# One diffusion layer in split fp32: weights stored in load order, and another opening order

## The chip, the cores and the metric

The kernel runs on one core of one Trainium2 chip. The metric is the device time of one execution in microseconds (us), the median of the runs shown. TensorE is called PE in the profile, VectorE DVE, ScalarE ACT, GpSimd POOL, SyncE SP; PEld is PE's weight load, which can run beside a matmul. SPq is SP's stream of issued transfers.

## The reference

One layer over 512 latent tokens and 128 context tokens, model width 1024. Cut to what the change touches:

```python
mod = (jax.nn.silu(cond) @ w_ada + b_ada)[:, None, :]
sh1, sc1, g1, sh2, sc2, g2 = jnp.split(mod, 6, axis=-1)
h = _rms(x, norm_mix) * (1 + sc1) + sh1
mix, k, v = _mixer(h, rope, ctx_k, ctx_v, w_in, q_norm, k_norm, conv_w,
                   attn_out_norm, conv_out_norm, w_out)
x = x + g1 * mix
h2 = _rms(x, norm_ffn) * (1 + sc2) + sh2
gate, up = jnp.split(h2 @ w_gate_up, 2, axis=-1)
x = x + g2 * ((jax.nn.silu(gate) * up) @ w_down)
```

`cond` is one vector for the latent tokens and another for the context tokens. The columns of `w_in` are q (512), k and v (256) and three blocks of 512 of a gated convolution. Inside `_mixer` stand attention (8 query heads, 2 key heads, one softmax over 640 keys) and the convolution.

## The kernel before, in words

**Arithmetic.** Every large product is made in three matmuls: an operand is split into a rounded part (`hH`, `wh`) and a rest (`hL`, `wl`), and `mm3` (lines 154 to 157) adds hH·wh, hH·wl and hL·wh in one PSUM bank. A weight tile of 128 partitions by 1024 floats (512 KB) is loaded into `wf`, rounded by ACT into `wh` (`w_hi`, line 542), and DVE makes `wl` (`w_lo`, line 549).

**Tiles.** There are five token tiles of 128 tokens, 0 to 3 latent, 4 the context. Eight slices `k` of 128 channels make the width.

**Stages.** The opening (0 to 59.6 us of the trace) loads the tokens, norms them, transposes them, makes the modulation of the first norm and computes q for all tiles. After it come keys and values, attention with the convolution's matmuls between (to about 250 us), the output projection, and the feed-forward part to the end. Only the opening's order of work is changed.

**The opening, step by step.** The string `P1SEQ` lists its steps by hand; PE, DVE, ACT, POOL and SP execute what they issue in that order, so an engine that waits at one step holds all its later ones. A digit is a tile or a slice:

- `r t`: ACT squares and sums token tile `x` (line 501), DVE scales the sum (L163), POOL takes the power -0.5 (L165). `s t`: DVE multiplies the tile by it (L507).
- `x t`: PE transposes the tile, eight blocks of 128x128 (L468). `e t i a|d`: ACT (L473) or DVE (L475) copies half `i` of it from PSUM to `xT`.
- `a k`: 16 small matmuls of the two conditioning vectors `cp` with the loaded slices `af` of `w_ada` (L394). `b k`: DVE copies the sum to `res` (L439). `m k`: two transposes (L446), a reduction (L448) and three small DVE operations make `modA` and `modB`, a scale and a shift per channel.
- `h k c`: ACT and DVE turn `xT` into `hH` and `hL` for all latent tiles (c=0) or the context tile (c=1) of slice k (L486 to L493, L151, L152).
- `q k t`: three matmuls of 512 columns for slice k and tile t (L155 to L157). `w`, `l`: rounding of the next weight tile. `d n`: n dummy matmuls on the identity (`spin`, L523). `v0`, `v1`: PE transposes bias, gain and filter vectors that POOL loaded as rows (L401, L553), DVE copies them to `vec`. `E t`: q of tile t leaves PSUM.

**Queues.** All large loads are issued by SP in the order of the string `LOADS` (x: a token tile, A: slices of `w_ada`, W: a weight tile, C: the cached keys and values). A transfer is cut into the runs that are contiguous in device memory: 4 KB per partition for a token tile, 512 bytes for `af`, the convolution's and the gate/up weights, 2 KB for q, `w_out` and `w_down`. `af` has four buffers (`AFB`), so the load of slice k+2 waits for step `a` of slice k; `wf` has three. At most eight transfers of SP are outstanding.

**PSUM.** In the opening, tag `s` has two buffers of two banks, `t` and `c` two banks each; one bank of `c` holds q of the context tile from first to last, so all `a` steps use the other.

Of the kernel before, what the change touches and what calls it, by code (L numbers as in the profile page):

```python
# [9 lines left out]
F32 = mybir.dt.float32  # L10
F32R = mybir.dt.float32r
AF = mybir.ActivationFunctionType
# [3 lines left out]
P = 128  # L16
D = 1024
# [15 lines left out]
P1SEQ = ('d11 r0 s0 x0 r1 s1 r2 e00d x1 s2 e01d r3 v0 d4 x2 s3 e20a a0 e10d b0 e11d e21d x3 m0 d4 w e30a h00y l n0 '  # L33
# [4 lines left out]
XB = 3  # L38
# [49 lines left out]
LOADS = 'xxxxAWxAAWAAWAAAWCWWWW'  # L88
# [3 lines left out]
def build(ctx, tc, x_prompt, x_sample, c, cache_k, cache_v, c_ctx, norm_mix, norm_ffn, w_ada, b_ada,  # L92
          w_in, q_norm, k_norm, conv_w, attn_out_norm, conv_out_norm, w_out, w_gate_up, w_down,
          rope_c, rope_s, o_prompt, o_sample, o_k, o_v):
# [43 lines left out]
    def PS2():  # L138
        return PB((P, 2, 512), tag="s")
# [33 lines left out]
    open_pool("B0", "left", "crow rows rows2 res x xT hF af")  # L173
# [5 lines left out]
    wi = w_in[0].rearrange("(k p) n -> p k n", p=P)  # L179
    wa = w_ada[0].rearrange("(k p) n -> p k n", p=P)  # L180
    wo = w_out[0].rearrange("(k p) n -> p k n", p=P)
    wg = w_gate_up[0].rearrange("(k p) n -> p k n", p=P)
    wd = w_down[0].rearrange("(k p) n -> p k n", p=P)
# [89 lines left out]
    for j in range(4):  # L273
        plan(("q", j), wi[:, 2 * j:2 * j + 2, O_Q:O_Q + 512])
    for h in range(2):
        plan(("kv", h), wi[:, 4 * h:4 * h + 4, O_K:O_K + 256])
    ada_steps = [(sec, j, h) for sec, j in ADA for h in range(4)]
    for n, (off, ct) in enumerate(CONV + [(None, 0)]):
        if off is not None:
            plan(("conv", off, ct), wi[:, :, off + ct * P:off + (ct + 1) * P])  # L280
        for sec, j, h in ada_steps[2 * n - 2:2 * n if off is not None else None] if n else ():
            col = sec * D + j * 512
            plan(("ada", sec, j, h), wa[:, 2 * h:2 * h + 2, col:col + 512], 1, "a")
    for j in range(2):
        for kp in range(4):
            plan(("o", j, kp), wo[:, 2 * kp:2 * kp + 2, j * 512:(j + 1) * 512], 2 * j, "w", V_AON + 2 * kp)
        for kp in range(0 if j else 4):
            plan(("ada", 5, j, kp), wa[:, 2 * kp:2 * kp + 2, 5 * D + j * 512:5 * D + (j + 1) * 512], 2, "f")
# [6 lines left out]
    def plan_raw(f, x, ph=3):  # L295
        col = f * P + (DFF if x == "u" else 0)
        plan((x, f), wg[:, :, col:col + P], ph, "f")
# [6 lines left out]
    for gi, grp in enumerate(GROUPS):  # L304
        for f in grp:
            ph = 2 if f < NPLAIN else 3
            plan_raw(f, "g", ph)
            plan_raw(f, "u", ph)
            plan_ops(f, PLAIN if f < NPLAIN else PRODS, ph)
        for j in range(2):  # L310
            for i0 in range(0, len(grp), 2):
                n = len(grp[i0:i0 + 2])
                plan(("d", grp[i0], j), wd[:, grp[i0]:grp[i0] + n, j * 512:(j + 1) * 512], 2)
                if gi == 0 and j == 0:
                    for kp in G2KP[i0 // 2]:
                        plan(("ada", 5, 1, kp), wa[:, 2 * kp:2 * kp + 2, 5 * D + 512:6 * D], 2, "f")


    crow = T("crow", (16, P))
    sp.dma_start(crow[0:8, :], c[0].rearrange("(r q) -> r q", q=P))  # L320
    sp.dma_start(crow[8:16, :], c_ctx.rearrange("(r q) -> r q", q=P))
# [20 lines left out]
    rows, rows2 = T("rows", (64, P)), T("rows2", (20, P))  # L342
    pool.dma_start(rows[0:48, :], b_ada[0].rearrange("(r q) -> r q", q=P))
    pool.dma_start(rows[48:56, :], norm_mix[0].rearrange("(r q) -> r q", q=P))
    pool.dma_start(rows[56:64, :], norm_ffn[0].rearrange("(r q) -> r q", q=P))
# [50 lines left out]
    vec = T("vec", (P, 84))  # L396
    nb = T("nb", (P, 2, KD))

    def vec_do():
        vps = PB((P, 64))  # L400
        pe.transpose(vps, rows, ident[:64, :64])  # L401
        dve.tensor_copy(vec[:, 0:64], vps)
# [60 lines left out]
    def xT_do(t):  # L463

        both = PS2() if t < XB else None
        xps[t] = [both[:, i] if t < XB else PB() for i in range(2)]
        for k in range(KD):
            pe.transpose(xps[t][k // 4][:, k % 4 * P:(k % 4 + 1) * P], xs[t][:, k * P:(k + 1) * P], ident)  # L468

    def xT_evict(t, i, e):  # L470
        dst, src = xT[:, 4 * i:4 * i + 4, t * P:(t + 1) * P], xps[t][i].rearrange("p (k q) -> p k q", q=P)
        if e == "a":
            act.activation(dst, src, AF.Copy)  # L473
        else:
            dve.tensor_copy(dst, src)  # L475
# [21 lines left out]

    def x_norm(t):
        junk = T2((P, D), mybir.dt.bfloat16)
        ss = T("ss", (P, 1), F32, 6)  # L500
        act.activation(junk, xs[t], AF.Square, accum_out=ss)
        rx[t] = rstd_of(ss, 1, 1.0 / D)
# [15 lines left out]
    done = {}  # L518

    def spin(n):  # L520

        for _ in range(n):
            pe.matmul(qacc[-1][:, :P], ident, ident, start=True, stop=True)  # L523
# [6 lines left out]
    def q_mm(k, t):  # L530
        if len(qacc) == 1:
            qa, qb = PS2(), PS2()
            qacc[:0] = [qa[:, 0], qa[:, 1], qb[:, 0], qb[:, 1]]
        wh, wl = W(("q", k // 2))
        s = slice(t * P, (t + 1) * P)
        mm3(qacc[t], hH[k][:, s], hL[k][:, s], wh[:, k % 2], wl[:, k % 2], *ends(t))
# [14 lines left out]
    def vec2_do():  # L551
        vps = PB((P, 20))
        pe.transpose(vps, rows2, ident[:20, :20])  # L553
        dve.tensor_copy(vec[:, 64:84], vps)

    gain_rows = {nm: T("gn" + nm, (P, HD)) for nm in "qk"}

    def rows2_load():
        for nm, g in (("q", q_norm), ("k", k_norm)):
            pool.dma_start(gain_rows[nm], g[0].partition_broadcast(P))  # L560
        pool.dma_start(rows2[0:4, :], attn_out_norm[0].rearrange("(r q) -> r q", q=P))
        pool.dma_start(rows2[4:8, :], conv_out_norm[0].rearrange("(r q) -> r q", q=P))
        pool.dma_start(rows2[8:20, :], conv_w[0].rearrange("w (r q) -> (w r) q", q=P))
# [3 lines left out]
    def rope_tables():  # L567
# [3 lines left out]
        pool.dma_start(rc, rope_c.rearrange("(t p) d -> p t d", p=P))  # L571
        pool.dma_start(rs_, rope_s.rearrange("(t p) d -> p t d", p=P))
# [17 lines left out]
    def q_evict(t):  # L590
        qraw[t] = T("of", (P, 512), F32, NT)
        if t == CTX:
            dve.tensor_copy(qraw[t], qacc[t])
        else:
            act.activation(qraw[t], qacc[t], AF.Copy)

    steps = {"r": x_norm, "s": x_scale, "c": late_consts, "w": w_hi, "l": w_lo, "p": lambda i: rows2_load(), "x": xT_do,
             "v": lambda i: (vec_do, vec2_do)[i](), "m": ada1_mod, "a": ada1_mm, "b": ada1_res, "d": spin,
             "n": h_rest, "E": q_evict, "R": lambda i: rope_tables()}
    in_pre[0] = True  # L600
    for x in P1SEQ.split():
# [728 lines left out]
    for n in ("psum", "G", "Y2", "Y1", "GT", "X", "A"):  # L1330
# [5 lines left out]
_INS = ["x_prompt", "x_sample", "c", "cache_k", "cache_v", "c_ctx", "norm_mix", "norm_ffn", "w_ada", "b_ada",  # L1336
        "w_in", "q_norm", "k_norm", "conv_w", "attn_out_norm", "conv_out_norm", "w_out", "w_gate_up", "w_down"]
# [19 lines left out]

# [23 lines left out]
```

## Time and profile before

| what | us |
| --- | --- |
| median of 3 runs (745.76 to 745.9) | 745.82 |
| the profiled execution, its own time | 747.05 |
| its span, first to last instruction | 745.2 |
| PE busy in the span | 729.4 |
| first transposition of a token tile | 8.17 |
| first matmul of q | 17.50 |
| first matmul of keys and values (the opening's end) | 59.61 |

Times in the prediction are in us from the start of the span. A row of the timeline or of the chain gives start, duration, engine, line, operation, output<-input and how many were merged; in square brackets how long the engine had been idle and who released it. A row of the table by windows gives for each engine its busy time and, in brackets, its instructions, then the granted clock, the DMA engines' busy share and GB/s.

### The profile page before, as it was taken

What the parts mean: (1) busy time and instruction counts of PE and PEld (TensorE: products, weight loads), DVE (VectorE), ACT (ScalarE), POOL (GpSimd) and SP (SyncE); (2) the same over time, 40 slices, a digit from 0 to 9 for tenths busy, and PEclk for the clock granted to TensorE, in tenths of its full rate; (3) what the DMA queues carried; (4) which work ended last, traced back from release to release, by engine and by line L of the source; (5) the groups of instructions that cost most, each with busy time, mean ns of one, the idle gap of its engine ahead of it and who ended that gap; (6) DMA issues with size and microseconds to landing.
All of it is one profiled execution on the core that took longest, in us unless ns stands there. A gap on an engine that the chain in (4) does not pass through costs nothing.

```text
span 745.2 us, 11646 instructions
## 1 busy us (share of the span) xinstructions
PE 729.4 (98%) x4556; PEld 658.8 (88%) x4556; DVE 530.3 (71%) x905; ACT 375.1 (50%) x701; POOL 49.0 (7%) x85
## 2 busy tenths in 40 slices
PE   7999899999999999999999999999999999999997
PEld 6568788999999887899998799998899998899986
DVE  5658878586667797888869767864668765677653
ACT  5357877777676544855552135552134541354510
POOL 2403100102010200100000000000000000000000
PEclk9999999999999999999999999999999999999999
DMA  9987152442341453122335314224014132123312
GB/s 289 295 240 228 43 170 65 148 150 83 131 149 49 150 171 113 30 85 57 114 100 187 96 32 111 77 94 142 28 57 113 57 114 86 56 74 97 105 66 85
DMA packets 101387, 84.50 MB, mean 113 GB/s; under 512 B 3502, under 2 KB 81650, under 8 KB 101332
## 3 DMA queue, kind: packets, MB, share of 16 engines
q1 hardware_dynamic: 100980, 83.39, 36.7%
q8 instruction: 36, 0.59, 0.3%
q0 software_dynamic: 352, 0.37, 0.3%
q14 instruction: 19, 0.16, 0.1%
HBM read 79.68 MB, written 2.75 MB: 111 GB/s over the span
## 4 chain that ended last, share of the span: by engine, by line
PE 84%; DVE 6%; DMA 4%; ACT 3%; issue 1%; POOL 1%; SPq 0%; ACTq 0%; DVEq 0%; POOLq 0%
PE pf L155 17%; PE pf L156 17%; PE pf L157 17%; PE pc L723 4%; PE pc L724 4%; PE pc L725 4%; PE po L878 3%; PE ps L834 3%; PE pt L861 2%; PE pc L394 2%; PE ph L156 2%; PE ph L157 2%; PE ph L155 2%; DMA wf<-in_w_gate_up_dram 2%; DMA af<-in_w_ada_dram 1%
## 5 line engine op out<-in xcount | busy, mean ns | idle before, releaser
L151 ACT ACTIVATE wh<-wf 128x1024 fp32r<-128x1024 f32 (+1 forms) x68 | 65.7, 970 | 106.8 <-PE pf L157 66.6
L152 DVE TENSOR_TENSOR wl<-wf,wh 128x1024 fp32r<-128x1024 f32 (+1 forms) x58 | 68.6, 1185 | 57.1 <-ACT wh L151 44.1
L157 PE MATMUL pf<-B,wl 128*128 128x320 f32 x288 | 89.2, 310 | 0.4 <-DVE wl L152 0.4
L155 PE MATMUL pf<-B,wh 128*128 128x320 f32 x288 | 89.1, 309 | 0.0
L156 PE MATMUL pf<-B,wh 128*128 128x320 f32 x288 | 89.0, 309 | 0.0
L155 PE MATMUL pf<-wh,gT 128*128 128x512 f32 (+1 forms) x225 | 86.9, 386 | 0.0
L155 PE MATMUL pf<-T,wh 128*128 128x320 f32 x280 | 86.7, 310 | 0.1
L156 PE MATMUL pf<-wl,gT 128*128 128x512 f32 (+1 forms) x225 | 86.5, 385 | 0.0
L157 PE MATMUL pf<-T,wl 128*128 128x320 f32 x280 | 86.5, 309 | 0.0
L156 PE MATMUL pf<-T,wh 128*128 128x320 f32 x280 | 86.5, 309 | 0.0
L157 PE MATMUL pf<-wh,gT 128*128 128x512 f32 (+1 forms) x225 | 86.5, 384 | 0.0
L151 ACT ACTIVATE wh<-sx 128x1024 fp32r<-128x1024 f32 x40 | 42.4, 1060 | 61.8 <-DVE sx L206 23.0
L152 DVE TENSOR_TENSOR wl<-sx,wh 128x1024 fp32r<-128x1024 f32 x40 | 49.0, 1225 | 28.0 <-ACT wh L151 24.4
L723 PE MATMUL pc<-hH,wh 128*128 128x320 f32 x192 | 60.9, 317 | 0.0
L725 PE MATMUL pc<-hH,wl 128*128 128x320 f32 x192 | 59.3, 309 | 0.0
L724 PE MATMUL pc<-hL,wh 128*128 128x320 f32 x192 | 59.3, 309 | 0.0
L157 PEld LDWEIGHTS pf<-B,wl 128*128 128x128 f32 x288 | 54.0, 188 | 0.8 <-DVE wl L152 0.7
L155 PEld LDWEIGHTS pf<-B,wh 128*128 128x128 f32 x288 | 54.1, 188 | 0.1
L156 PEld LDWEIGHTS pf<-B,wh 128*128 128x128 f32 x288 | 54.1, 188 | 0.1
L155 PEld LDWEIGHTS pf<-T,wh 128*128 128x128 f32 x280 | 52.5, 188 | 0.6 <-ACT u L1211 0.4
L156 PEld LDWEIGHTS pf<-T,wh 128*128 128x128 f32 x280 | 52.6, 188 | 0.0
L157 PEld LDWEIGHTS pf<-T,wl 128*128 128x128 f32 x280 | 52.6, 188 | 0.0
(302 smaller groups left out, 1671.1 us busy)
## 6 DMA issues: line engine op xcount, KB each, us to landing
wf<-in_w_gate_up_dram SPq DMA_DIRECT2D x44, 512.0 KB, 4.2
aw<-in_w_ada_dram SPq DMA_DIRECT2D x24, 512.0 KB, 6.3
wf<-in_w_down_dram SPq DMA_DIRECT2D x20, 512.0 KB, 3.5
wf<-in_w_in_dram SPq DMA_DIRECT2D x18, 512.0 KB, 6.5
af<-in_w_ada_dram SPq DMA_DIRECT2D x32, 256.0 KB, 6.4
x<-in_x_sample_dram SPq DMA_DIRECT2D x8, 512.0 KB, 6.0
wf<-in_w_out_dram SPq DMA_DIRECT2D x8, 512.0 KB, 3.4
wf<-in_w_ada_dram SPq DMA_DIRECT2D x8, 512.0 KB, 3.8
```

The source lines that it names most:

```text
L151: act.activation(hi, src, AF.Copy)
L152: dve.tensor_tensor(lo, src, f32(hi), ALU.subtract)
L155: pe.matmul(out, lh, rh, start=start, stop=False, skip_group_check=more)
L156: pe.matmul(out, lh, rl, start=False, stop=False, skip_group_check=more)
L157: pe.matmul(out, ll, rh, start=False, stop=stop, skip_group_check=more)
L394: pe.matmul(out[CG * g:CG * (g + 1)], cp[:, k], w, start=(k < 4), stop=(k >= KD - 4), skip_group_check=True)
L723: pe.matmul(acc, wh[:, k], hH[k][:, c0:c0 + n], start=(k == 0), stop=False)
L724: pe.matmul(acc, wh[:, k], hL[k][:, c0:c0 + n], start=False, stop=False)
L725: pe.matmul(acc, wl[:, k], hH[k][:, c0:c0 + n], start=False, stop=(k == KD - 1))
L834: pe.matmul(s2[:, g, :320], q, kk[:, v, P + g * 320:P + (g + 1) * 320], start=(i == 0), stop=(i == 1))
L861: pe.transpose(tp[:, i, h], u[3][h][:, kt * P:(kt + 1) * P], ident)
L878: pe.matmul(ov, w, x[:, i].rearrange("p a q -> p (a q)"), start=(g == 0 and i == 0 and n == 0), stop=(last and i == len(kts) - 1 and n == 1))
```

## The change

**Layout.** The host reorders the arrays before the launch, outside the measured time (`_layout`): each tile that one load fetches is stored as one block of 128 rows of 4 KB (for `w_down` rows of 4 KB at a larger pitch, and 2 KB for the last odd tile of a group). The two `af` loads of 256 KB per buffer become one of 512 KB. The conditioning vectors and all bias, gain and filter vectors come transposed, so `crow` and `vec` are each one load by SP, and the PE transpositions L382, L401 and L553, their DVE copies and six row loads by POOL are gone. The two rope tables are one load.

**Opening order.** `P1SEQ` and `LOADS` are new, and so is a step `g`; `x` now takes half a tile at a time:

```diff
-P1SEQ = ('d11 r0 s0 x0 r1 s1 r2 e00d x1 s2 e01d r3 v0 d4 x2 s3 e20a a0 e10d b0 e11d e21d x3 m0 d4 w e30a h00y l n0 '
-         'r4 q01 e31d s4 q02 a1 x4 b1 e40d m1 h01x h10 q00 a2 b2 h11 q04 m2 w e41a q03 l q10 h20 q11 q12 h21 q13 q14 a3 b3 '
...
-         'm7 h70 h71 q60 q61 w l q62 q63 q64 w l q70 q71 E0 E1 q72 q73 E2 E3 q74 E4 w l')
-XB = 3
+P1SEQ = ('r0 d9 s0 x00 x01 e00a a0 e01a b0 v0 w m0 r1 g00 l r2 s1 q00 s2 x11 e11d x20 e20d x10 r3 e10d a1 r4 '
+         'g02 g01 s4 x21 b1 q02 x40 s3 e21a q01 x30 e40a g04 m1 e30a g03 h10x q04 n1 w x41 e41d a2 x31 q11 '
...
+         'h61 R q64 b7 m7 q42 w q60 h70 q53 l q61 q63 h71 q70 q71 q62 w l E0 E1 q74 l q73 E4 q72 E2 w l E3')
+XB = 1
-LOADS = 'xxxxAWxAAWAAWAAAWCWWWW'
+LOADS = 'xAWxxxxAAWAAWAWAWAWCWW'
@@
-            for i, col in enumerate((D + k * P, k * P)):
-                sp.dma_start(wf[:, :, i], wa[:, 4 * h:4 * h + 4, col:col + P])
+            sp.dma_start(wf, w_mod[k, h])
@@
-    act.activation(crow, crow, AF.Silu)
-    cps = PB((P, 16))
-    pe.transpose(cps, crow, ident[:16, :16])
-    cs = T("cs", (P, KD, 2))
-    dve.tensor_copy(cs, cps.rearrange("p (c k) -> p k c", c=2))
+    cs = T("cs", (P, KD, 2))
+    act.activation(cs, craw, AF.Silu)
@@
+    def h_tile(k, t):
...
+        act.activation(hH[k][:, s], xT[:, k, s], AF.Identity, bias=b, scale=a)
+        dve.tensor_scalar(hF[k][:, s], xT[:, k, s], a, b, ALU.mult, ALU.add)
+        dve.tensor_tensor(hL[k][:, s], hF[k][:, s], f32(hH[k][:, s]), ALU.subtract)
@@
+    a["w_mod"] = ada[:, :, 1::-1].reshape(2, 4, P, 2, KD, P).transpose(4, 0, 2, 1, 3, 5)
+    a["w_gate_up"] = w["w_gate_up"][0].reshape(KD, P, 2, NF, P).transpose(2, 3, 1, 0, 4)
```

Slice 0 is thus made tile by tile (`g0t`), and the first q steps stand between the transpositions. The dummy matmuls go from 11+4+4 to 9, all ahead of the first tile.

**The order on the engines.** SP, the first loads before; `x` are token tiles, `af` slices of `w_ada`, `wf` a weight tile:

```order
L320 DMA crow_74<-in_c_dram 8x128
L321 DMA crow_74<-in_c_ctx_dram 8x128
L352 DMA x_96<-in_x_sample_dram 128x1024
L352 DMA x_98<-in_x_sample_dram 128x1024
L352 DMA x_100<-in_x_sample_dram 128x1024
L352 DMA x_102<-in_x_sample_dram 128x1024
L329 DMA af_104<-in_w_ada_dram 128x4x128 x2
L329 DMA af_107<-in_w_ada_dram 128x4x128 x2
L228 DMA wf_110<-in_w_in_dram 128x2x512
```

and now:

```order
L313 DMA crow_74<-in_cond_dram 128x16
L315 DMA vec_76<-in_vectors_dram 128x84
L342 DMA x_92<-in_x_sample_dram 128x1024
L323 DMA af_94<-in_w_mod_dram 128x1024
L323 DMA af_96<-in_w_mod_dram 128x1024
L223 DMA wf_98<-in_w_q_dram 128x1024
L342 DMA x_100<-in_x_sample_dram 128x1024
L342 DMA x_102<-in_x_sample_dram 128x1024
L342 DMA x_104<-in_x_sample_dram 128x1024
```

The first token tile keeps its place; the data of `a0` and the first q weights have moved ahead of tiles 1 to 3.

PE, from its first row, before (`ps` and `pt` receive transposed tokens, `pc_211` the dummies, `pc_296` step `a0`):

```order
L382 MATMUL pt_179<-ident_77,crow_74 128x16
L523 MATMUL pc_211<-ident_77 128x128 x11
L468 MATMUL ps_233<-ident_77,x_96 128x128 x8
L468 MATMUL ps_258<-ident_77,x_98 128x128 x8
L401 MATMUL pt_276<-ident_77,rows_87 128x64
L523 MATMUL pc_211<-ident_77 128x128 x4
L468 MATMUL ps_285<-ident_77,x_100 128x128 x8
L394 MATMUL pc_296<-af_104,cp_85 32x256 x4
```

and now, to the fifth half tile (`pc_187` the dummies, `pc_217` step `a0`, `ps_262` q of tile 0):

```order
L517 MATMUL pc_187<-ident_78 128x128 x9
L452 MATMUL ps_207<-ident_78,x_92 128x128 x8
L379 MATMUL pc_217<-af_94,cp_86 32x256 x4
L379 MATMUL pc_217<-af_96,cp_86 32x256 x4
L426 MATMUL pc_234<-ident_78,res_227 128x128 x2
L154 MATMUL ps_262<-wh_231,hH_48_169 128x512
L155 MATMUL ps_262<-wl_232,hH_48_169 128x512
L156 MATMUL ps_262<-wh_231,hL_56_177 128x512
L452 MATMUL pt_267<-ident_78,x_100 128x128 x4
L452 MATMUL pt_273<-ident_78,x_102 128x128 x4
L452 MATMUL pt_279<-ident_78,x_100 128x128 x4
L379 MATMUL pc_292<-af_108,cp_86 32x256 x4
```

Step `a0` and one q step now stand ahead of the second tile's transposition; the eight dummies in between are gone.

DVE, from the modulation of slice 0 on, now (`ms` belongs to the norms of tiles 1 and 2, `wl_232` to the first q weights):

```order
L401 TENSOR_TENSOR modB_46_167<-modt_237,vec_76 128x2
L162 TENSOR_SCALAR ms_245<-ss_243 128x1
L489 TENSOR_SCALAR hF_249<-xT_185,modA_44_165,modB_46_167 128x128
L490 TENSOR_TENSOR hL_56_177<-hF_249,hH_48_169 128x128
L544 TENSOR_TENSOR wl_232<-wf_98,wh_231 128x1024
L162 TENSOR_SCALAR ms_257<-ss_255 128x1
L501 TENSOR_SCALAR x_100<-x_100,rs_247 128x1024
L501 TENSOR_SCALAR x_102<-x_102,rs_259 128x1024
L459 COPY xT_185<-pt_267 128x4x128
```

The norms of tiles 1 and 2, which stood ahead of the modulation, now stand behind it, and behind the 1024-wide `wl`. From the first matmul of keys and values on, all five engines issue the same operations in the same order as before.

More of the change, by code (lines that the diff above doesn't have):

```diff
@@ L172, in build @@
     open_pool("B1", "left", "t2 tab selT identr ck cv gnq gnk")
-    open_pool("B0", "left", "crow rows rows2 res x xT hF af")
+    open_pool("B0", "left", "crow res x xT hF af")
     open_psum("pp1", {"t": 2, "c": 2, "s": 2})
@@ L312, in build @@
                 n = len(grp[i0:i0 + 2])
-                plan(("d", grp[i0], j), wd[:, grp[i0]:grp[i0] + n, j * 512:(j + 1) * 512], 2)
+                plan(("d", grp[i0], j), w_down[j][:, grp[i0]:grp[i0] + n], 2)
                 if gi == 0 and j == 0:
                     for kp in G2KP[i0 // 2]:
[L316 to L321, printed above, removed]
+                        plan(("ada", 5, 1, kp), w_ada[3, 1, kp], 2, "f")
+    craw = T("crow", (P, KD, 2))
+    sp.dma_start(craw, cond)
+    vec = T("vec", (P, 84))
+    sp.dma_start(vec, vectors)
     def ada1_load(k):
@@ L341, in build @@
     pool.memset(cp, 0.0)
[L342 to L345, printed above, removed]
     xs = []
@@ L461, in build, with xT_do @@
     xps = {}
[L463 to L468, printed above, removed]
+    def xT_do(t, i):
+        if t < XB and i == 0:
+            xps[t, 1] = PS2()
+            xps[t, 0], xps[t, 1] = xps[t, 1][:, 0], xps[t, 1][:, 1]
+        elif t >= XB:
+            xps[t, i] = PB()
+        for k in range(4):
+            c0 = (4 * i + k) * P
+            pe.transpose(xps[t, i][:, k * P:(k + 1) * P], xs[t][:, c0:c0 + P], ident)
     def xT_evict(t, i, e):
-        dst, src = xT[:, 4 * i:4 * i + 4, t * P:(t + 1) * P], xps[t][i].rearrange("p (k q) -> p k q", q=P)
+        dst, src = xT[:, 4 * i:4 * i + 4, t * P:(t + 1) * P], xps[t, i].rearrange("p (k q) -> p k q", q=P)
         if e == "a":
@@ L496, in h_do @@
             split(hH[k], hL[k], hF[k])
+    def h_tile(k, t):
+        if k not in hF:
+            hF[k] = T("hF", (P, TOK), F32, 2)
+        s = slice(t * P, (t + 1) * P)
+        cc = int(t == CTX)
+        a, b = modA[0][:, k, cc:cc + 1], modB[0][:, k, cc:cc + 1]
+        act.activation(hH[k][:, s], xT[:, k, s], AF.Identity, bias=b, scale=a)
+        dve.tensor_scalar(hF[k][:, s], xT[:, k, s], a, b, ALU.mult, ALU.add)
+        dve.tensor_tensor(hL[k][:, s], hF[k][:, s], f32(hH[k][:, s]), ALU.subtract)
     def x_norm(t):
@@ L517, in build @@
     qacc = [PB(tag="c")]
-    done = {}
+    done, qps = {}, {}
     def spin(n):
         for _ in range(n):
-            pe.matmul(qacc[-1][:, :P], ident, ident, start=True, stop=True)
+            pe.matmul(qacc[0][:, :P], ident, ident, start=True, stop=True)
     def ends(key):
@@ L530, in q_mm @@
     def q_mm(k, t):
-        if len(qacc) == 1:
-            qa, qb = PS2(), PS2()
-            qacc[:0] = [qa[:, 0], qa[:, 1], qb[:, 0], qb[:, 1]]
+        if t < CTX and t not in qps:
+            two = PS2()
+            qps[t // 2 * 2], qps[t // 2 * 2 + 1] = two[:, 0], two[:, 1]
+        acc = qps.setdefault(t, qacc[0])
         wh, wl = W(("q", k // 2))
         s = slice(t * P, (t + 1) * P)
-        mm3(qacc[t], hH[k][:, s], hL[k][:, s], wh[:, k % 2], wl[:, k % 2], *ends(t))
+        mm3(acc, hH[k][:, s], hL[k][:, s], wh[:, k % 2], wl[:, k % 2], *ends(t))
     def w_hi(_):
@@ L606, in build @@
             q_mm(k, int(x[2]))
+        elif x[0] == "g":
+            h_tile(k, int(x[2]))
+        elif x[0] == "x":
+            xT_do(k, int(x[2]))
         elif x[0] == "e":
```

79 lines of the change are left out of this document (37 added, 42 removed), and 4 rows, old and new, of the table P1SEQ.

## The prediction

> **What bounds the kernel.** I read the page's busy times and slices first, then the table by windows, then the timeline of the opening, then the chain of waits for two late places.
>
> ```profile
> span 745.2 us, 11646 instructions
> PE 729.4 (98%) x4556; PEld 658.8 (88%) x4556; DVE 530.3 (71%) x905; ACT 375.1 (50%) x701; POOL 49.0 (7%) x85
> PE   7999899999999999999999999999999999999997
> DMA  9987152442341453122335314224014132123312
> ```
>
> PE is busy for all but 15.8 us. DMA is full only in the first four slices (75 us). Where the 15.8 us lie, and what the opening holds:
>
> ```profile
> 8.15:20.05 11.90, 9.87 (x73) 7.08 (x73) 10.14 (x25) 6.30 (x10) 2.62 (x5) 1.00 1.14 323
> 20.05:59.60 39.55, 38.60 (x250) 25.55 (x250) 24.59 (x65) 19.26 (x27) 7.77 (x17) 1.00 0.99 272
> 59.60:130.00 70.40, 66.57 (x493) 59.49 (x492) 56.99 (x139) 53.23 (x127) 11.37 (x16) 1.00 0.38 115
> 270.00:330.00 60.00, 58.67 (x308) 49.56 (x307) 50.85 (x76) 37.27 (x82) 3.09 (x5) 1.00 0.30 88
> 30.96 0.64 PE L394 MATMUL pc<-af,cp 128*32 128x256 f32 x8 [0.49 <-DMA af<-in_w_ada_dram]
> 34.26 0.64 PE L394 MATMUL pc<-af,cp 128*32 128x256 f32 x8 [0.27 <-DMA af<-in_w_ada_dram]
> 59.61 0.28 PE L155 MATMUL pc<-wh,hH 128*128 128x256 f32 x1
> ```
>
> From 20.05 to 59.60, DMA is saturated (0.99), yet PE idles only 39.55 - 38.60 = 0.95 us, of which DMA is named for 0.49 + 0.27 = 0.76. So a faster load can return about 0.8 us there, not more. From 8.15 to 20.05 PE idles 2.03 us and spends more on dummies. Everything behind 59.61 is the same program, moved by as much as this matmul moves, plus what late waits give back.
>
> **The first tile: nothing.** Its way to the first transposition:
>
> ```profile
> 1.54 1.78 SPq L352 DMA_DIRECT2D x<-in_x_sample_dram  x4
> 5.34 1.06 ACT L501 ACTIVATE t<-x 128x1024 bf16<-128x1024 f32 x1 [2.44 <-DMA x<-in_x_sample_dram]
> 6.88 1.06 ACT L501 ACTIVATE t<-x 128x1024 bf16<-128x1024 f32 x1 [0.39 <-DMA x<-in_x_sample_dram]
> 7.37 0.75 DVE L507 TENSOR_SCALAR x<-x,rs 128x1024 f32<-128x1024 f32 x1 [0.69 <-POOL rs L165]
> 8.17 1.10 PE L468 MATMUL ps<-ident,x 128*128 128x128 f32 x8
> ```
>
> The tile is SP's third load before and after, behind two small ones, so I keep 8.17, with 0.5 us either way (behind it now come weights instead of tiles; `vec`, 43 KB, is new ahead of it). The vanished transposition of `crow` and the POOL loads lie ahead of 8.17, covered by the tile's flight.
>
> **How fast the loads land.** Tiles with 4 KB rows and slices with 512-byte rows, each alone in the queue:
>
> ```profile
> 7.00:8.00 1.00, 1.00 (x6) 0.88 (x5) 0.64 (x1) 1.00 (x2) 0.33 (x1) 1.00 1.05 420
> 16.00:20.00 4.00, 2.48 (x11) 1.31 (x9) 3.76 (x11) 2.32 (x4) 0.93 (x2) 1.00 1.20 290
> ```
>
> 512 KB take 1.25 us at 420 GB/s; the second tile landed 6.88 - 5.34 = 1.54 after the first. I take 1.25 to 1.54 per load, all having 4 KB rows now. By position, counting from 5.34: `a0`'s data by 7.8 to 8.4, the q weights 9.1 to 10, tile 1 at 10.3 to 11.5, `a1`'s data (tenth) at 16.6 to 19.2.
>
> [...]
>
> **The new opening, walked.** Durations:
>
> ```profile
> 13.24 0.60 ACT L473 ACTIVATE xT<-ps 128x512 f32<-128x512 f32 x1 [2.03 <-PE ps L468]
> 14.92 1.06 ACT L542 ACTIVATE wh<-wf 128x1024 fp32r<-128x1024 f32 x1 [1.08 <-DMA wf<-in_w_in_dram]
> 14.38 0.42 DVE L439 COPY res<-pc 128x256 f32<-128x256 f32 x1 [0.31 <-PE pc L394]
> 15.18 0.38 PE L446 MATMUL pc<-ident,res 128*128 128x128 f32 x2
> 15.92 0.16 DVE L448 TENSOR_REDUCE modt<-pc 128x4 f32<-128x16 f32 x1
> 16.39 0.15 DVE L421 TENSOR_TENSOR modB<-modt,vec 128x2 f32<-128x2 f32 x1
> 17.11 1.22 DVE L549 TENSOR_TENSOR wl<-wf,wh 128x1024 fp32r<-128x1024 f32 x1
> 20.11 1.07 PE L394 MATMUL pc<-af,cp 128*32 128x256 f32 x16
> 23.48 0.31 ACT L151 ACTIVATE hH<-hF 128x128 fp32r<-128x128 f32 x1 [4.98 <-DVE hF L492]
> 23.82 0.29 DVE L152 TENSOR_TENSOR hL<-hF,hH 128x128 fp32r<-128x128 f32 x1 [0.38 <-ACT hH L151]
> 28.21 0.34 DVE L492 TENSOR_SCALAR hF<-xT,modA,modB 128x128 f32<-128x128 f32 x1
> ```
>
> PE: tile 0 from 8.17, `a0` 9.2 to 10.3, DVE `res` to 10.7, two transpositions to 11.2, the reduction to `modB` 16.39 + 0.15 - 15.92 = 0.62, so 11.8. Meanwhile ACT copies both halves (to 10.0), rounds the q weights (to 11.1), and then stands at the square of tile 1 (1.06, with its read of the sum 1.25): to 12.3, and only then `hH`, to 12.6. So q's first matmul comes at 12.65, 0.8 after `modB`, held by that square. DVE waits for the same square, then makes hF, hL, and `wl`: 12.35 + 0.15 + 0.34 + 0.29 + 1.22 = 14.4; q's second matmul waits for it, 1.5 us, and q ends at 14.9. The scaling of tiles 1 and 2 (0.75 each) is queued behind `wl`: half tiles at 15.3, 16.1 and 16.8. `a1` starts at 17.3 if its data is there (16.6 to 19.2) and ends at 18.4, or at 19.8 with a slow queue.
>
> **The balance there.** Before, at 20.05, PE has done eight half tiles, `a0` and two q steps. In the new order at 18.4: five half tiles, `a0`, `a1`, one q step. Missing are three half tiles (0.5 each) and one q step (0.7) less `a1` (1.07): 1.1 us. Dropping eight dummies and moving three tiles back has thus gained 20.05 - 18.4 - 1.1 = **0.5 us**, or lost 0.9 with the slow queue. The gain is small because the place of the dummies and tiles is taken by the waits of 1.5, 1.5 and 0.4 us on the chain above.
>
> **From there to keys and values.** Gone: the 0.76 us on DMA and, with the last transposition of vectors, about 0.3. New: tiles 3 and 4 are scaled late on DVE (tile-wise slice 0 gives it five times 0.34 + 0.29 instead of one 512-wide pair and one context pair, about 1.2 us more), which I estimate to hold PE 0.7 us in all around tile 4, q3 and q7, bounded by 0 and that 1.2; and half tiles between q steps restart the stream about seven times more. A restart costs 0.1 us by the first matmul behind another kind:
>
> ```profile
> 17.50 0.51 PE L155 MATMUL ps<-wh,hH 128*128 128x512 f32 x1 [1.05 <-ACT hH L486]
> 29.07 0.39 PE L155 MATMUL pc<-wh,hH 128*128 128x512 f32 x1
> ```
>
> 0.51 against 0.39; seven make 0.8. Sum: -1.1 + 0.7 + 0.8 = **+0.4 us**, ends -1.1 and +0.9. The opening as a whole: -0.5 + 0.4 = -0.1, taken as **0**, ends -2.1 (both best, the tile 0.5 sooner) and +2.3.
>
> **Behind 59.61.** Faster landings matter only where PE waited for a load's consequences:
>
> ```profile
> 278.21 3.33 DMA wf<-in_w_out_dram
> 312.83 4.61 DMA wf<-in_w_gate_up_dram
> ```
>
> The second, with 512-byte rows, would take about as long as the first with its 2 KB rows, 1.3 us less, but PE idles only 1.33 us in all between 270 and 330. I take **-0.4 us**, ends 0 and -1.3. Between 59.6 and 130 the 3.8 us of idling belong to operations of DVE and ACT that do not change. The other weights land ahead of use; halving their flight is worth nothing.
>
> **Sum.** 0 - 0.4: the span 745.2 becomes 744.8, the profiled execution's 747.05 becomes 746.65, and the median 745.82 becomes **745.4**.
>
> **Rivals.**
>
> *The waits close.* If tile 0 lands 0.5 us sooner (it no longer shares the queue with three tiles) and DVE's extra work hides, the opening gives 2.1 and the late waits 0.4: 743.3. For it: PE does 0.95 us of idling from 20 to 60 under a saturated queue. Against: the chain through `modB`, the square and `wl`, which no load shortens. It needs over 1.1 us in the opening.
>
> *PE stays at half speed* (slower). The dummies show two paces:
>
> ```profile
> 3.20 4.88 PE L523 MATMUL pc<-ident 128*128 128x128 f32 x22
> 15.40 1.06 PE L523 MATMUL pc<-ident 128*128 128x128 f32 x8
> ```
>
> 22 in 4.88 is 0.22 us each, 8 in 1.06 is 0.13 with the drain in it; tile 0's eight, right behind the first row, take 1.10. So PE sped up about when the 22 ended, though the granted clock is printed as 1.00 all along. Now there are 18, four us worth, then 2 us of nothing, and no later dummies in a stretch with only 3 us of work between 8.2 and 14.9. If 18 do not suffice, tile 0 and `a0` take double (2.1 us), and then PE needs some 4.9 us of dense work at half pace before it speeds up (2.4): 745.4 + 4.5 = 749.9; half of it, if `a0` wakes it, 747.6. It decides at the pace of `a0`: 1.07 or 2.1.
>
> [...]
>
> *The layout does nothing for landing.* Then 290 GB/s hold, 1.8 us per load: `a1` waits until 21.5, and the DMA waits stay; about +2 on the opening, hidden in part: 746.5 to 747.5.
>
> **Chances.** Forecast, 744.4 to 746.6: 0.42. Waits close: 0.27. Half speed: 0.22. No faster loads: 0.09, of which 0.04 above 747.3. Within 0.2% (1.5 us, about what a measurement of this kernel can tell from no change) is 744.33 to 747.31: 0.42 + 0.05 - 0.01 = 0.46; faster 0.27 + 0.01 = 0.28; slower 0.22 + 0.04 = 0.26. The range leaves out the fastest of the first rival and the worst of half speed: 743.2 to 749.0; the likeliest case alone has 744.4 to 746.6.
>
> **What will show it.** Tile 0's transposition near 8.2; `a0` at 1.07 us and not 2.1; q's first matmul near 12.7 released by ACT's `hH`, its second near 14.5 by DVE's `wl`; no wait of PE for `af`; SP's queue near 400 GB/s to 45 us; the first matmul of keys and values near 59.6. A first q matmul near 14.9 or `a0` over 1.6 means the clock; keys and values before 58.3 means that I mis-sized DVE's share.

## The result, and the profile after

The changed kernel took 750.83 us (median of 4 executions, 750.57 to 751.02), the kernel before 745.79 beside it: a ratio of 1.0069, 95% interval 1.0051 to 1.0086. It is **5.0 us slower**. The forecast was 745.4 and its range ended at 749.0; both were too low. The profiled execution took 750.57 us with a span of 748.8, 3.6 over the span before; the profiled execution of before lay 1.2 us over its own median, which makes up most of the rest.

The page's header, and two rows of the slices (40 equal ones, tenths busy):

```profile
span 748.8 us, 11554 instructions
PE 732.8 (98%) x4533; PEld 657.9 (88%) x4533; DVE 529.6 (71%) x908; ACT 376.8 (50%) x706; POOL 47.1 (6%) x78
PE   6999899999999999999999999999999999999997
DMA  8855142343341452111336121324113141122312
```

PE does 23 fewer instructions and is busy 3.4 us **longer**, so it did not wait more (its idle time is 16.0 us, 15.8 before): it worked more slowly. The windows (span, busy time of each engine, granted clock, DMA share, GB/s) say the same:

```profile
8.15:19.90 11.75, 9.18 (x41) 5.51 (x41) 5.88 (x17) 6.75 (x13) 1.64 (x2) 1.00 1.02 411
19.90:60.67 40.77, 39.92 (x264) 28.00 (x264) 29.67 (x77) 21.75 (x31) 8.78 (x15) 1.00 0.73 250
273.00:333.00 60.00, 59.59 (x319) 50.75 (x318) 49.53 (x74) 38.18 (x83) 3.09 (x5) 1.00 0.23 80
```

DMA moved 411 GB/s where it moved 323 before, and PE idles 0.41 us of the late stretch where it idled 1.33. Both went as the change meant them to. The opening on PE's timeline:

```profile
1.58 4.21 PE L517 MATMUL pc<-ident 128*128 128x128 f32 x18 [1.58 <-POOL ident masks.py:199]
8.18 1.97 PE L452 MATMUL ps<-ident,x 128*128 128x128 f32 x8 [2.40 <-DVE x L501]
10.07 1.94 PE L379 MATMUL pc<-af,cp 128*32 128x256 f32 x16
14.56 0.79 PE L154 MATMUL ps<-wh,hH 128*128 128x512 f32 x1 [1.32 <-ACT hH L488]
16.02 0.80 PE L155 MATMUL ps<-wl,hH 128*128 128x512 f32 x1 [0.67 <-DVE ms L162]
17.05 2.96 PE L452 MATMUL pt<-ident,x 128*128 128x128 f32 x12
19.93 1.22 PE L379 MATMUL pc<-af,cp 128*32 128x256 f32 x16
60.67 0.28 PE L154 MATMUL pc<-wh,hH 128*128 128x256 f32 x1
```

The tile lands when it did, but its eight transpositions take 1.97 us in place of 1.10 and `a0` 1.94 in place of 1.07. That is half pace, up to about 20 us, while the clock is printed as 1.00. Keys and values start at 60.67, 1.06 late. That is under a third of the 3.6 us of span. The rest lies where the forecast saw nothing. These are the first matmul of the down projection (on `gT`) and the last matmul of the program, before:

```profile
392.29 0.39 PE L155 MATMUL pf<-wh,gT 128*128 128x512 f32 x1
740.92 0.28 PE L157 MATMUL pf<-wh,gT 128*128 128x256 f32 x1
```

and after:

```profile
391.57 0.40 PE L154 MATMUL pf<-wh,gT 128*128 128x512 f32 x1
744.38 0.28 PE L156 MATMUL pf<-wh,gT 128*128 128x256 f32 x1
```

At the down projection the changed kernel is 0.72 us *ahead*; at the end it is 3.46 behind. In between, the two programs hold the same instructions in the same order, and PE is busy without a break in both, as the window between the landmarks shows, before and after:

```profile
392.29:740.92 348.63, 348.63 (x2025) 322.42 (x2023) 235.73 (x330) 129.51 (x200) 0.00 (x0) 1.00 0.29 87
```

```profile
391.57:744.38 352.81, 352.81 (x2024) 322.10 (x2023) 233.70 (x325) 128.83 (x199) 0.00 (x0) 1.00 0.26 86
```

(The one matmul less in the second row is the last, which starts just behind the window's rounded edge.) Yet it takes 352.81 us in place of 348.63. Nineteen neighbouring rows of that stretch show how, first before, then after:

```profile
404.78 0.39 PE L156 MATMUL pf<-wl,gT 128*128 128x512 f32 x1
405.01 0.39 PE L157 MATMUL pf<-wh,gT 128*128 128x512 f32 x1
...
408.86 0.39 PE L156 MATMUL pf<-wl,gT 128*128 128x512 f32 x1
```

```profile
404.64 0.39 PE L156 MATMUL pf<-wh,gT 128*128 128x512 f32 x1
404.87 0.39 PE L154 MATMUL pf<-wh,gT 128*128 128x512 f32 x1
...
408.84 0.39 PE L156 MATMUL pf<-wh,gT 128*128 128x512 f32 x1
```

The duration of one is the same, 0.39; only the start of the next tells. Eighteen steps take 4.08 us before and 4.20 after: **226.7 and 233.3 ns for one matmul** of 512 columns. The program has 645 of them on `gT`: 645 x 6.7 ns = 4.3 us, against 4.18 by the landmarks. Matmuls of 320 columns keep their pace, 146.7 ns from start to start in both. Those of 256 columns come quicker in after, every 114 ns and not every 120; keys and values have 120 of them, and the 30 of the down projection take some 0.2 us off the 4.3.

What differs for these matmuls is where their operand stands. Pool A hands out places in the order of first use. Before, `m0` came ahead of `w` in the steps, so the two 32-byte buffers of `modt` (in `mod_sum`) got byte 19008 of each partition, and the four buffers each of `wh` and `wl` began at 19072. Now `w` stands ahead of `m0`, and `wh` begins at 19008: 64 bytes lower (the places are those of the built program's table of tiles; no trace shows them). `hH`, `mx`, `sx` and `gT`, from which TensorE loads its weights while `wh` and `wl` stream, are where they were, 128 bytes over a multiple of 256.

### The profile page after: what moved, and what is told of

The parts are those of the page before. It is cut to its first block, busy times and chain, and to the rows that moved or that the text cites. A ratio compares the mean times of both kernels' runs of the same rounds, so it can differ in the third digit from the quotient of the medians.

```text
span 748.8 us, 11554 instructions
## 1 busy us (share of the span) xinstructions
PE 732.8 (98%) x4533; PEld 657.9 (88%) x4533; DVE 529.6 (71%) x908; ACT 376.8 (50%) x706; POOL 47.1 (6%) x78
## 3 DMA queue, kind: packets, MB, share of 16 engines
HBM read 79.68 MB, written 2.75 MB: 110 GB/s over the span
## 4 chain that ended last, share of the span: by engine, by line
PE 87%; DVE 7%; ACT 2%; issue 1%; DMA 1%; POOL 1%; SPq 0%; DVEq 0%; ACTq 0%
PE pf L156 19%; PE pf L154 19%; PE pf L155 19%; PE pc L713 4%; PE pc L714 4%; PE pc L715 4%; PE ps L824 3%; PE po L868 2%; PE pt L851 2%; PE pc L379 2%; PE ph L155 1%; PE ph L156 1%; PE ph L154 1%; PE ps L155 1%; PE ps L156 1%
## 5 line engine op out<-in xcount | busy, mean ns | idle before, releaser
L154 PE MATMUL pf<-wh,gT 128*128 128x512 f32 (+1 forms) x225 | 88.1, 391 | 0.0
L156 PE MATMUL pf<-wh,gT 128*128 128x512 f32 (+1 forms) x225 | 87.6, 389 | 0.0
```

The lines of the kernel that those rows point to most:

```text
L154: pe.matmul(out, lh, rh, start=start, stop=False, skip_group_check=more)
L156: pe.matmul(out, ll, rh, start=False, stop=stop, skip_group_check=more)
```

## The experiments

Three theories were tried. A: the place of `wh` and `wl` sets the pace of the 512-column matmuls. B: only the half pace of the opening matters. C: the longer rows of the new layout disturb TensorE. Each time below stands beside executions of the kernel before on the same chip, whose medians were 745.79 (beside after), 746.38 (e1 to e4), 746.32 (e6 to e8) and 746.25 (e9 to e12). Three landmarks of the profiles, in us, with each kernel's median and its ratio to before. The landmarks are of one profiled execution, which need not be near the median: it took 745.60 in e6, 745.71 in e9, 748.27 in e12.

| kernel | keys and values start | from there to `gT` | from `gT` to the last matmul | median | ratio (interval) |
|---|---|---|---|---|---|
| before | 59.61 | 332.68 | 348.63 | | |
| after | 60.67 | 330.90 | 352.81 | 750.83 | 1.0069 (1.0051 to 1.0086) |
| e11, after again | 60.55 | 331.60 | 352.81 | 750.86 | 1.0052 (1.0039 to 1.0066) |
| e1, weights back | 60.79 | 330.52 | 348.80 | 746.09 | 0.9993 (0.9984 to 1.0002) |
| e2, more dummies | 59.30 | 331.65 | 352.82 | 749.53 | 1.0042 (1.0028 to 1.0055) |
| e3, both | 60.13 | 330.55 | 348.80 | 745.11 | 0.9983 (0.9975 to 0.9992) |
| e4, before shifted | 59.60 | 332.52 | 349.93 | 747.72 | 1.0018 (1.0009 to 1.0026) |
| e6, layout, old order | 59.40 | 331.47 | 348.64 | 748.14 | 1.0017 (1.0007 to 1.0027) |
| e7, dummies in the gap | 58.43 | 330.63 | 348.79 | 744.97 | 0.9983 (0.9974 to 0.9991) |
| e8, square later | 59.59 | 330.99 | 348.79 | 745.24 | 0.9988 (0.9979 to 0.9997) |
| e9, e6 with more dummies | 59.70 | 331.29 | 348.63 | 747.02 | 1.0003 (0.9993 to 1.0013) |
| e10, candidate | 59.16 | 330.66 | 348.78 | 744.16 | 0.9971 (0.9959 to 0.9982) |
| e12, old order, no gap dummies | 60.52 | 333.08 | 348.64 | 747.07 | 1.0011 (1.0002 to 1.0020) |

### The place

**e1, weights back.** `modt` takes its two buffers first, as before the change:

```diff
+    for _ in range(2):
+        T("modt", (P, 2, 2), F32, 2)
     xT = T("xT", (P, KD, TOK))
```

> After, with the two modt buffers allotted before the first wh and wl, so that wh and wl stand at byte 19072 (a multiple of 128) as before the change and not at 19008; steps, loads and all that is computed stay. Theory A (place): a 512-column matmul that streams wh or wl starts every 233 ns in after and every 227 ns in before, because the tiles moved by 64 bytes. 861 such matmuls lie behind the opening (645 on gT, 216 in the output projection, without 24 that were slow before too), 120 in it; 6.7 ns each is 5.7 and 0.6 us. The pace of all of them returns to 227 ns; some of it may be taken by waits that come back: 750.8 becomes 744.4 to 746.5. Theory B (only the half pace of the opening matters): the pace stays at 233 ns and the time at 750.8. Theory C (the longer rows of the new layout disturb TensorE's reads): the same, 750.8.

746.09: the whole loss to within the interval is gone with 64 bytes. The steps of the pace:

```profile
404.71 0.39 PE L156 MATMUL pf<-wh,gT 128*128 128x512 f32 x1
...
408.79 0.39 PE L156 MATMUL pf<-wh,gT 128*128 128x512 f32 x1
```

Eighteen steps take 4.08 us again, though the rows of the layout are as long as in after. B and C fall; the opening is as slow as in after (60.79).

**e4, before shifted.** The same from the other side, on the kernel before:

```diff
-PLACE = 48, 72
+PLACE = 32, 72
...
+    T("padW", (P, 16))
     xT = T("xT", (P, KD, TOK))
```

> Before, with 64 bytes of padding ahead of modt, wh and wl and 64 fewer behind them, so that wh and wl stand at byte 19136 (64 over a multiple of 128) and all tiles of later pools where they were; the program's order and loads stay. Theory A (place): the 512-column matmuls start every 233 ns in place of 227, up to 957 times 6.7 ns: 745.8 becomes 750.5 to 752.0. Theories B and C: 745.8, since neither the opening nor the loads change.

747.72, only 1.3 over before, where A wanted 4.7 to 6.2. The pace had changed, but little:

```profile
404.70 0.39 PE L156 MATMUL pf<-wl,gT 128*128 128x512 f32 x1
...
408.82 0.39 PE L156 MATMUL pf<-wl,gT 128*128 128x512 f32 x1
```

4.12 us for 18 are 228.9 ns (228.3 in the text below): neither 227 nor 233. So "a multiple of 128" was the wrong rule: 64 bytes up costs 2 ns, 64 bytes down 6.7.

**e5, address sweep.** TensorE alone, nothing else running:

```python
for i in range(n):
    pe.matmul(o, sta[:, so:so + P], mov[:, mo:mo + w], start=i == 0, stop=i == n - 1)
...
for mo in range(0, 513, 8):
    mark()
    run(N, 32, mo, 512)
for so in (48, 120, 128, 64):
    for mo in range(0, 128, 8):
        mark()
        run(N, so, mo, 512)
```

> TensorE alone: nothing of the kernel's result is computed. Rows of 18 matmuls with 512 moving columns (fp32r, weights loaded again for each, as in the kernel), the moving tile's start in SBUF stepped by 32 bytes, the weights' start at a remainder of 128 by 512 as in the kernel, then at 192, 480, 0 and 256; then rows with 320 and 256 columns. Theory A1 (the start address alone sets the pace): what the kernels showed comes again, 226.7 ns at a remainder of 128, 228.3 at 192, 233.3 at 64, and the sweep shows the rule; 18 matmuls take 4.08, 4.11 and 4.20 us and the drain. Weights at 480 (as tile m) give 233.3. Theory A2 (the address matters only through other engines or DMAs that touch SBUF at the same time): all rows alike.

Four of its groups of 18, all with the weights at 128 over a multiple of 512, and the streamed tile at 0, 64, 128 and 192:

```profile
18.55 4.43 PE L39 MATMUL a<-mov,sta 128*128 128x512 f32 x18
...
27.16 4.44 PE L39 MATMUL a<-mov,sta 128*128 128x512 f32 x18
...
35.77 4.37 PE L39 MATMUL a<-mov,sta 128*128 128x512 f32 x18
...
44.30 4.38 PE L39 MATMUL a<-mov,sta 128*128 128x512 f32 x18
```

And with the weights at 192, the streamed tile at 128 and at 192:

```profile
314.45 4.44 PE L39 MATMUL a<-mov,sta 128*128 128x512 f32 x18
...
323.06 4.34 PE L39 MATMUL a<-mov,sta 128*128 128x512 f32 x18
```

With the weights at 192 the quick place has moved to 192. So A2 falls, for the rows differ with nothing else running, and A1 falls in its letter, for the start of the streamed tile alone does not decide. In this sweep what counts is the **distance** from the weights' place to the streamed tile's, in bytes modulo 256. Over all 129 groups of 512 columns, from one group's start to the next (a small matmul stands between them): distance 0 takes 4.20 to 4.24 us, 64 takes 4.24 to 4.25, and every other multiple of 32 takes 4.28 to 4.34. With 320 columns all take 2.75 or 2.76. With 256 it is turned round, 2.26 at distance 0 and 2.23 to 2.25 elsewhere. The kernels agree: distance 0 in before and e1 (226.7), 64 in e4 (228.9), 192 in after (233.3); tile `m` of the output projection, 224 over a multiple of 256, ran at 233 in before too. The matmuls of 256 columns are turned round in the kernels as well: 120 ns at distance 0, 118 at 64 (e4), 114 at 192. In size the sweep does not repeat the kernel: it has 4 to 6 ns between best and worst where the kernel has 6.7, and its best, some 233 ns from start to start within a group, is the kernel's worst. So it shows that the distance counts and which one is quick, not the kernel's figures; why they differ is open.

### The pace of the opening

**e2, more dummies.** `d9` becomes `d15`.

> After with 30 dummy passes ahead of the first tile in place of 18, nothing else. Theory B (half pace): the pace changes after some 22 passes, so they end near 7.5 and tile 0 takes 1.1 us, a0 1.07, the first q matmul comes at 12.7 in place of 14.56, a1 at 17.3 in place of 19.93; keys and values start at 58.2 to 58.8 in place of 60.67, and the time falls by 1.9 to 2.5 us, to 748.3 to 748.9. If B were the whole of the loss, it would fall by 4.5 to 5. Theory A (place): the 512-column pace stays at 233 ns, so at most the opening's part is won and the rest of the 5.0 us stays. If the dummies were no cause: 750.8, or up to 751.7 where they run over into tile 0.

749.53, ratio 1.0042 against after's 1.0069 and 1.0052: 0.7 to 2.0 us gained, at or under the low end of what B gave. Its timeline, and two windows:

```profile
1.58 5.12 PE L517 MATMUL pc<-ident 128*128 128x128 f32 x30 [1.58 <-POOL ident masks.py:199]
8.39 1.09 PE L452 MATMUL ps<-ident,x 128*128 128x128 f32 x8 [1.69 <-DVE x L501]
9.41 1.07 PE L379 MATMUL pc<-af,cp 128*32 128x256 f32 x16
```

```profile
12.00:15.00 3.00, 0.89 (x3) 0.48 (x3) 2.42 (x8) 3.00 (x8) 0.89 (x2) 1.00 1.04 421
16.00:18.00 2.00, 1.92 (x10) 1.52 (x9) 1.48 (x3) 0.08 (x1) 0.00 (x0) 0.50 1.02 406
```

Too few dummies are the cause of the first half pace: now tile 0 and `a0` run at full pace. But PE is busy for only 0.89 of the 3 us from 12 to 15, and from 16 to 18 the granted clock reads 0.50: it fell again behind the thin stretch. **e3**, e1 and e2 together:

> After with both edits: wh and wl at a multiple of 128 again, and 30 dummy passes. If the two causes are independent the gains add up: e1's 4.3 to 6.4 and e2's 1.9 to 2.5 give 741.9 to 744.6, below the kernel before the change. Theory B alone: as e2. Place alone: as e1.

745.11, under before by 0.17%: place and dummies do add up, 4.4 us from e2 to e3 and 1.0 from e1 to e3 (the intervals of e1 and e3 overlap). It missed its forecast by 0.5; like e2 it falls back:

```profile
16.39 1.97 PE L454 MATMUL pt<-ident,x 128*128 128x128 f32 x8 [0.54 <-DVE x L503]
18.29 1.94 PE L379 MATMUL pc<-af,cp 128*32 128x256 f32 x16
```

**e7, dummies in the gap.** e3 with `d17`, and `m0 d6 r1 g00` for `m0 r1 g00`.

> e3 with 34 dummy passes ahead of tile 0 in place of 30 and 12 more behind m0, where TensorE waits 1.5 us for hH. In e3 TensorE fell back to half pace from 16.4 to 22.5 us; if the thin stretch from 11 to 16 us did that, the half pace goes: keys and values start at 58.4 to 59.4 in place of 60.1, and the time falls by 0.7 to 1.7 from e3's 745.1, to 743.4 to 744.4. If the fall back has another cause: 745.1, within 0.4.

The profile is as forecast, the clock stays at 1.00 (8 to 24 us) and keys and values start at 58.43:

```profile
11.25 1.50 PE L519 MATMUL pc<-ident 128*128 128x128 f32 x12
12.96 0.50 PE L154 MATMUL ps<-wh,hH 128*128 128x512 f32 x1 [0.21 <-ACT hH L490]
17.66 1.07 PE L379 MATMUL pc<-af,cp 128*32 128x256 f32 x16
```

The profiled execution took 744.19, but the median is 744.97, only 0.14 under e3, with a spread from 743.87 to 745.85. **e10**, with `d19` ahead of tile 0 and `d2` behind tile 1's first half:

> e7 with 38 passes ahead of tile 0 in place of 34, and 4 more behind tile 1's first half, where TensorE waits 0.5 us for the scaled tile. If the spread of e7's times (743.9 to 745.9) comes from half pace in some executions, the median falls to 743.8 to 744.5 with a narrower spread; if TensorE was always at full pace in e7: as e7, 745.0, or 0.2 to 0.4 more.

744.16, from 743.56 to 745.13: 0.29% under the kernel before and 0.9% under the change, the best median of all, though its interval overlaps e7's. Half pace can have made only part of e7's spread. The four of its eleven executions whose granted clock reads 0.996 to 0.998 in the mean have spans of 742.9 to 744.0, the other seven 742.1 to 742.9, and e10 has 0.999 or 1.000 in all six. But in e7 up to 2.8 us of the time lie outside the span, where every other kernel has 1.7 to 1.9; why is open. By the medians of the spans, 742.7 in e7 and 743.3 in e3, the further dummies gained 0.6 us and not 0.14. Nor is full pace all: e10's profiled execution had it and took 744.76, with tile 0 transposed only at 9.24, 0.9 later than in e7.

**e8, square later.** e3 with `d17`, and `m0 g00 l r1 r2` for `m0 r1 g00 l r2`.

> e3 with 34 dummy passes ahead of tile 0 and the square of tile 1 moved behind g00 and the low part of the q weights, so that ACT does not stand at it when hH is wanted. If that square holds q's first matmul, it comes at about 12.1 in place of 12.9, released by DVE's modB, and the time falls by 0.3 to 0.8 us to 744.3 to 744.8, unless tile 1's half, now later, gives it back: then 745.1 or more.

745.24, no gain. The first q matmul came at 12.60 in place of 12.88: the square held it by 0.3 us, not by 0.8. At keys and values e8 is 0.5 us ahead of e3 (59.59 against 60.13), and it loses 0.4 of that on the way to `gT`.

**e12, old order without gap dummies.** The kernel before, both `d4` taken out.

> The kernel before the change without its two rows of 8 dummy passes between tiles 1 and 2 and ahead of the first q matmul; the first row of 22 stays. If dummies in the gaps keep the pace up: some of tile 2, a0, tile 3 and q's first step run at half pace, keys and values start 1 to 3 us later than 59.61, and the time is 0.8 to 2.8 us more. If they are only filler: the same time within 0.3, or up to 1 us less, since the first row of 8 takes 1.16 us of TensorE's time ahead of tile 2.

747.07, 0.8 over before, at the low edge of the forecast; the interval begins just above no change. The clock falls in this order too, though not where the forecast had it: tile 2, `a0` and tile 3 still run at full pace, and the fall comes behind them.

```profile
18.00:20.00 2.00, 1.95 (x4) 1.44 (x5) 1.93 (x4) 0.16 (x2) 1.25 (x2) 0.50 1.20 290
```

```profile
20.66 1.94 PE L394 MATMUL pc<-af,cp 128*32 128x256 f32 x16
```

So the eight dummies (two rows of eight passes) that the forecast counted as gained by leaving them out were worth keeping: without them 9 of 11 executions have a mean clock of 0.998 or less, with them 8 of 22. They do not hold the old opening at full pace every time. e4 has them, and its profile reads 0.50 too:

```profile
18.75:22.17 3.42, 3.42 (x20) 1.59 (x20) 1.26 (x2) 0.00 (x0) 3.42 (x6) 0.50 1.29 271
```

### The layout with the old order

**e6.** After's code with the steps (`x0` as `x00 x01`, without `v1`), `XB` and `LOADS` of before.

> The new layout in device memory with the old order: steps, order of loads and the three tiles with whole steps as before the change, only the first row of dummies 30 passes long in place of 22, since it starts 1.6 us sooner; wh and wl then stand at 19072 as before. If the layout is worth what e1 and e3 showed behind the opening (2.0 us from waits of 60 to 362 us) and takes the two waits on DMA in the opening (0.76 us): keys and values start at 58.6 to 59.3 and the time is 2.0 to 3.1 us under the kernel before, 743.3 to 744.4 beside 746.4. If those waits closed because of the new order and not of the layout: within 0.8 of 746.4.

The row of dummies was in fact left at 22 passes, against its description. They now begin 1.6 us sooner, since no transposition of `crow` is waited for, and end sooner:

```profile
1.58 4.24 PE L513 MATMUL pc<-ident 128*128 128x128 f32 x22 [1.58 <-POOL ident masks.py:199]
8.40 3.52 PE L448 MATMUL ps<-ident,x 128*128 128x128 f32 x16 [2.58 <-DVE ms L158]
11.76 1.06 PE L513 MATMUL pc<-ident 128*128 128x128 f32 x8
```

22 passes at the cold pace of after (4.21 / 18 = 0.234) would be 5.15 us, so in 4.24 PE had already sped up; after 2.58 us of nothing it is back at half pace (the clock reads 0.57 from 8 to 12 us, 1.00 before and behind), and by the end of the transpositions, 3.36 us from their start, it has sped up again: the eight dummies behind them take 1.06. The times fall into two groups, five of 745.60 to 746.51 and seven of 748.12 to 749.19. The one profile is of the first group and all twelve have a mean clock of 0.994 to 0.998, so what parts the groups is not shown.

**e9.** e6 with `d17`.

> e6 with the first row of dummies 34 passes long (in e6 it was still 22, against its description: they ended 1.6 us sooner than before the change, TensorE then stood idle for 2.6 us, and the first two tiles ran at half pace). If the half pace made e6's 748.1: tile 0's eight transpositions take 1.1 us, keys and values start at 58.3 to 59.3, the later waits give 1.3, and the time is 1.2 to 2.4 us under the kernel before on the same chip. If the layout with the old order is worth nothing: within 0.5 of before.

747.02, no different from before: the forecast of 1.2 to 2.4 us under it fails. The profiled execution, 745.71, was at full pace and shows what the layout gives: 1.4 us from keys and values to `gT`, and nothing ahead of them (59.70). The other executions run up to 748.97; their mean clocks are 0.994 to 0.998 where the four best have 0.999 or 1.000, so the clock falls in them too. Those seven average 747.5 us, the four 745.5. The kernel before is not free of the fall either: 8 of its 22 executions on this chip have 0.996 to 0.998, yet they average 746.5 against 746.4 for the rest. Why a fall costs 2 us with the new layout in this order, and next to nothing with the old one, stays open.

**e11**, after once more:

> The changed kernel once more, beside the others on one chip: 750.5 to 752, 4.5 to 5.5 us over the kernel before.

750.86. From `gT` on its profile takes the same 352.81 us as after. The opening is not the same from execution to execution: here `a0` took 1.52 us, not 1.94, and the clock reads 0.50 from 14.4 to 21.2 and once more from 72.4 to 75.8.

## Why the prediction was wrong, point by point

- **The step that failed** was "Everything behind 59.61 is the same program, moved by as much as this matmul moves". The order was the same, the places of the operands were not. It cost 4.2 us from `gT` on (352.81 against 348.63), and about 1.2 more in the output projection, 216 matmuls of 512 columns at 233 ns in place of 227 to 228, of which the quicker matmuls of keys and values gave back about 0.5. e1 takes it away with 64 bytes and brings back 226.7 ns; e4 and e5 show that place alone changes the pace. Neither the forecast nor a rival had it.
- **The first tile: nothing.** Right in after (8.18) and e11 (8.10), but 0.5 us was too narrow: 8.94 in e9's profile, 9.24 in e10's.
- **How fast the loads land.** Right where it mattered: 411 GB/s up to `a1`, and PE never waited for `af`, so the rival of no faster loads falls. The sign of 400 GB/s up to 45 us did not come: from 19.9 to 60.67 it is 250, for SP had to wait until PE had used its `af` buffers (17.1 us in that stretch, five waits for `pc` of the `a` steps).
- **The walk.** It took full pace; after ran at half until 20 us. For a PE at full pace it was right to 0.4 us: in e7 q's first two matmuls came at 12.96 and 14.56 (12.65 and 14.4 forecast), `a1` at 17.66 (17.3). One reason in it was off: the square held `hH` by 0.3 (e8).
- **From there to keys and values.** Too dear. At full pace (e7) keys and values start 39.7 us after the end of `a1`, where 41.1 follow from the forecast, so the term is -1.0 and not +0.4. The 0.7 for DVE was there, as one wait for tile 4:

```profile
20.69 0.63 PE L454 MATMUL pt<-ident,x 128*128 128x128 f32 x4 [0.67 <-DVE x L503]
```

So the 0.8 for restarts, or another part of that bookkeeping, was too dear; which, no run shows. Keys and values start 1.2 us sooner than before, where the opening was put at 0; 1.2 lies within the ends given.
- **Behind 59.61: -0.4, ends 0 and -1.3.** Too small. With the weights in their place it is 330.5 to 331.0 us from keys and values to `gT` with the new order, 1.7 to 2.2 less than before. The layout alone gives 1.2 to 1.4 (e6, e9); the rest comes with the order. One wait that goes in e1, though its operations were not touched, is this one of before, which the forecast counted as unchanged; in e6 it is still there with 0.6 us, so it goes with the order and not with the layout:

```profile
90.34 0.41 PE L834 MATMUL ps<-KB,qT 128*128 128x320 f32 x1 [0.71 <-DVE KB L670]
```

- **PE stays at half speed.** The half pace was there, and `a0` at 1.94 decided it as said. The price of 4.5 was too high: dummies return 1.0 us (e1 to e3) to 1.8 (e1 lies 0.3 under before, e10 2.1). From tile 0 to q's first matmul after takes 1.8 us longer than e7, near the 2.1 for tile 0 and `a0`. From there to `a1` it takes only 0.7 longer, and that is the term that was mis-sized: 2.4 for 4.9 us of dense work at half pace, in a stretch that is thin. That 749.9 came near 750.8 was chance: nearly all of the difference was the place.
- **The waits close: 743.3.** With place and clock held (e10) the change gives 2.1 us, 744.2 beside 746.25. So order and layout earned 2.1, the lost dummies took 1.0 to 1.8, and the place 4.4 (e2 to e3) to 4.9 (e1 to e11): together 3.3 to 4.6 against the 4.6 (e11) and 5.0 measured, so by this sum, whose terms come from different chips, the costs lie near their upper ends.

## What to carry to other kernels

A step that is moved can also move tiles: where a pool hands out places by first use, compare the addresses of the operands of the most frequent matmuls in both builds, and compare their pace by the distance between starts, not by durations. In these runs the dummies that keep TensorE busy had to last nearly until the real work: where they ended 1.24 to 1.90 us ahead of tile 0 it ran at full pace (e7, e10, e2, e9), where they ended 2.58 us ahead it did not (e6). They also had to fill the gaps behind it: with 12 passes behind `m0` the clock stayed at 1.00 (e7), without them it read 0.50 from 16 to 22 us (e3). The longest rows and the most gaps filled (e10) gave the best median, 744.16, and even so e9 shows executions in which the clock fell (seven of eleven, 0.994 to 0.998 in the mean). A profile that shows more busy time with fewer instructions asks for the pace of one kind of instruction, stage by stage, before anything about waits.

## What the runs showed of the hardware

- A 512-column fp32r matmul started every 226.7 (before, e1), 228.9 (e4) or 233.3 ns (after), by the distance modulo 256 between the places of streamed tile and weights (0, 64, 192); in e5, alone, 18 of them took 4.20 to 4.24 us at distance 0, 4.24 to 4.25 at 64 and 4.28 to 4.34 at the others. With 320 columns there was no difference (146.7 in before and after, 2.75 or 2.76 us for 18 in e5), and with 256 the order was turned round (120 in before, 118 in e4, 114 in after).
- In these profiles the printed clock shows half pace only from a first change on. In after it reads 1.00 all along while 16 passes of `a0` take 1.94 us, and in e11 1.00 from 8 to 12 us while tile 0 takes 1.97; in e2 and e12 it reads 0.50 after a fall. So a higher mean can belong to the slower execution: e1's five with 1.000 took 746.19 to 746.57 us, its six with 0.993 to 0.995 took 744.81 to 746.09. The pace of a known instruction decides.
- TensorE was back at half pace after 2.58 us of idling (e6: the 16 transpositions behind it took 3.52 us, the clock reads 0.57 from 8 to 12 us), and still at full pace after 1.90 (e9: eight transpositions in 1.09). In e2 it fell at the end of a stretch in which it was busy for 0.89 us of 3 (12 to 15 us, clock 1.00; 0.50 from 16 to 18); the longest idle time in that stretch was 1.55 us. In e6 nothing but transpositions ran on PE from 8.40 to 11.76, and the dummies behind them took 1.06 for eight, full pace: transpositions alone had sped it up.
